# Feed-forward chunks of a four-layer trunk: the narrow chunk moved to the front, all five wide chunks in seven block products

## The chip, the cores and the metric

The kernel runs on one core of one Trainium2 chip. The metric is device time in microseconds (us), lower is better. A core has five engines that run their own instruction streams in order: PE (matmul; its weight loads, PEld, overlap it), DVE (element-wise, two tensors in), ACT (element-wise, one tensor in), POOL and SP; here POOL and SP mainly issue DMAs. What is queued on an engine behind a waiting instruction waits too.

## What is computed

A trunk of four layers on 256 tokens of width 1024, all in float32. Each layer is a feed-forward block (FFN), an attention block and a second FFN; so there are eight FFNs, and the change touches only them. Cut to that:

```
D_MODEL = 1024; SEQ = 256; DEPTH = 4; D_FF = 2816

def swiglu(x, w_in, w_out):
    gate, up = jnp.split(x @ w_in, 2, axis=-1)
    return (jax.nn.silu(gate) * up) @ w_out

for i in range(DEPTH):
    h = h + 0.5 * rms_norm(swiglu(rms_norm(h, g[0]), ffn_w_in[i, 0], ffn_w_out[i, 0]), g[1])
    ... attention: h = h + rms_norm(m, g[3])
    h = h + 0.5 * rms_norm(swiglu(rms_norm(h, g[4]), ffn_w_in[i, 1], ffn_w_out[i, 1]), g[5])
return h
```

## The kernel before

**Three passes for one product.** PE multiplies in a reduced form of float32 (fp32r), so every operand is split into a high part `hi` and a remainder `lo`, and a product is summed from three passes: x_hi·w_hi, x_hi·w_lo, x_lo·w_hi (`product`, L152; in the output products L244 to L246). The split of a weight unit of 128x2048 elements is one cast on ACT (L156, `hi`) and one subtraction on DVE (L157, `lo`). Weights come by DMA into "raw" tiles (nine, `RAWS`), and the split pairs stand in a ring of four (`UNITS`).

**Tokens.** The 256 tokens are two tiles, t=0 and t=1. Before an FFN each tile's normalized input (`xg`) is turned on PE (L181, `tpx`) and split into `xh` (ACT) and `xl` (DVE); ACT also copies the turned tile back (L184).

**Chunks.** The 2816 hidden columns are done in six chunks: five of 512 and one of 256. A chunk needs, for gate and up and for both token tiles, a product over the 1024 inputs. `plain` does these four products as they stand: 96 matmuls, of 512 or 256 columns. `wino` does the 2x2x2 block product (two token tiles, two input halves, gate and up) in seven block products of 12 matmuls (84) after Strassen and Winograd. For it, four sums of x (L271 to L274, `early`) and sums of the four weight quarters b00, b01, b10, b11 are formed: two of the weight sums on DVE (L372, 128x2048 each), two by accumulating DMAs that POOL issues (L375). The products of a wino chunk come in the order b00, b10, t2, t1, t3, b11, t4, into three PSUM banks `pb`, `pa`, `pc`; ACT copies the running sums out of `pb` (L492, L504, L509), DVE adds `pa` and `pc` (L487) and forms the gated value `g` (L431). `g` is turned (L439, `tpg`), split into `gh` (ACT) and `gl` (DVE), and multiplied into the output sums `y` one chunk later.

**Order before.** Chunk 0 is a plain 512, chunk 1 the plain 256, chunks 2 to 5 are wino 512s. The turn of token tile 1 (`turn_x`) stands in the second product of chunk 0, and the sums of x follow its third. The order in which each engine meets the instructions is set by a scheduler that works from its own estimates, not by the program text; so it is read from the built program.

The FFNs are called FFN 1 to FFN 8 in the order in which they run. FFN 3, 5 and 7 follow an FFN, FFN 2, 4, 6 and 8 an attention.

Of the kernel before, what the change touches and what calls it, by code (L numbers as in the profile page):

```python
# [9 lines left out]
F32 = mybir.dt.float32  # L10
# [26 lines left out]

RAWS = 9
UNITS = 4
WINO = (2, 3, 4, 5)  # L40

IN_NAMES = ["x", "norm_g", "ffn_w_in", "ffn_w_out", "diff_w_in", "diff_w_out", "diff_lambda",
            "diff_subln", "moba_w_in", "moba_w_out", "nsa_w_in", "nsa_w_out", "nsa_cmp_pe",
# [3 lines left out]
class Trunk:  # L47
# [235 lines left out]
    def ffn(self, l, f, X, ahead, end):  # L283
        nc = self.nc
        with self.tc.tile_pool(name=f"ffn{l}{f}", bufs=2, reuse_waits="tile") as pool:
            w_in, w_out = self.a["ffn_w_in"][l, f], self.a["ffn_w_out"][l, f]
            chunks = [(c, 512) for c in range(0, D_FF - 256, 512)]
            chunks.insert(1, (D_FF - 256, 256))
            last = len(chunks) - 1
            y = [None, None]  # L290
            G, U = {}, {}
# [45 lines left out]
            def close(n):  # L337
                U.pop(n)
                live["unit"] -= 1
# [19 lines left out]
            def plan_wino(j):  # L359


                c0, w = chunks[j]
                name = lambda n: (j, n)
                quarter = lambda k, u: (w_in, k * 512, 4, u * D_FF + c0, w)
                c1, w1 = chunks[j - 1]
                ko = [((j - 1, "o", k), (w_out, c1 + k * P, 2, 0, D)) for k in range(0, w1 // P, 2)]
                for n, src in ((name("b00"), quarter(0, 0)), (name("b01"), quarter(0, 1)),
                               (name("b10"), quarter(1, 0)), (name("b11"), quarter(1, 1)), (name("t2"), None), *ko):
                    loads.append(lambda n=n, src=src: raw(n, src))

                def add(to, a, b):
                    nc.vector.tensor_tensor(R[name(to)], R[name(a)], R[name(b)], op=ALU.add)  # L372

                def add_by_dma(to, b):
                    nc.gpsimd.dma_start(R[name(to)], R[name(b)], accum_op=ALU.add)  # L375

                def quarters(n, then=()):
                    split(name(n), name(n))
                    for x in then:
                        (add if len(x) == 3 else add_by_dma)(*x)  # L380

                def last_of(n, of, gone=None):
                    split(name(n), name(of), True)
                    if gone:
                        free(name(gone))

                outs = [lambda n=n: split(n, n, True) for n, _ in ko]

                def split_t2():
                    add("t2", "b00", "b11")  # L390
                    quarters("t2", [("t2", "b10")])

                preps.extend([
                    lambda: quarters("b00"),
                    lambda: quarters("b10", [("b00", "b00", "b01"), ("b01", "b11")]),
                    outs[0],
                    split_t2,
                    lambda: last_of("t1", "b00"),
                    lambda: last_of("t3", "b01"),
                    lambda: last_of("b11", "b11")])  # L400
                if j < last:
                    preps.extend(outs[1:])
                preps.append(lambda: last_of("t4", "t2", "b10"))
                if j == last:
                    preps.extend(outs[1:])

# [45 lines left out]
            def plain(j, order, between=()):  # L452
# [4 lines left out]
                for i, (which, t) in enumerate(order):  # L457
                    ns = [(j, "gu"[which], h) for h in hs]
                    ps = bank("ps")
                    for h, n in zip(hs, ns):  # L460
                        self.product(ps[:, :w], X[t][0], [(4 * h, unit(n))], h == 0, h == hs[-1])
                        if i == 1:
                            self.turn_x()
                    if which == 0:
                        sl[t] = gate(t, ps, w, j)
                    else:
                        up(t, ps, w, sl[t], j, X[t][1])
                    if (which, 1 - t) in order[:i]:
                        for n in ns:
                            close(n)  # L470
                    fill()
                    if between:
                        between.pop(0)()

            def wino(j):
# [9 lines left out]

                tile = lambda tag, t: pool.tile([P, 512], F32, tag=tag, name=f"{tag}{l}{f}_{j}_{t}")
                add = lambda d, x: nc.vector.tensor_tensor(d, x, d, op=ALU.add)  # L487
                s24, s31 = SUMS
                B = bank("pb")
                times(B, X[0][0], 0, "b00", True)  # L490
                sl0 = tile("sl", 0)
                nc.scalar.copy(sl0, B)  # L492
                fill()
                turn(j - 1, 0)
                A = bank("pa")
                times(A, X[0][0], 4, "b10", True)
# [47 lines left out]
                    nc.vector.tensor_scalar(r, X[t][1], -1.0, None, op0=ALU.mult)  # L544
                    nr.append(r)

            plain(0, [(0, 0), (1, 0), (0, 1), (1, 1)], [lambda: None, lambda: None, early])
            zig = [(0, 0), (0, 1), (1, 0), (1, 1)]
            for j in range(1, last + 1):
                if j in WINO:  # L550
                    wino(j)
                    continue
                plain(j, zig, [lambda: turn(j - 1, 0), lambda: turn(j - 1, 1)])
                for t in range(NT):
                    out(j - 1, t, (0, 2))
                for k in (0, 2):
                    close((j - 1, "o", k))
                fill()
                del G[j - 1, 0], G[j - 1, 1]
            turn(last, 0)  # L560
            out(last - 1, 0, (2,))
            ahead()
# [768 lines left out]
```

## Time and profile before

| | before |
|---|---|
| median of 3 runs | 1992.58 us (1991.72 to 1995.25) |
| the profiled execution, its own time | 1992.68 us |
| its span in the profile | 1991.0 us |
| PE busy | 1934.5 us (97%) |
| DVE busy | 1610.7 us (81%) |
| ACT busy | 1261.7 us (63%) |
| granted TensorE clock, mean | 0.999 |

The span is what the profile shows of one execution; 1.7 us of the execution's time lie around it. An engine's share is a mean over stages: PE can be the limit in one stretch and wait in another, and the stages of one FFN are told apart by time below.

### The profile page before, as it was taken

The page shows a single profiled execution, that of the slowest core. Times are in us where ns is not written, and L with a number is a line of the kernel's source. Part 1 is how long each engine was busy: PE and PEld are TensorE (multiplying, and loading weights), DVE is VectorE, ACT ScalarE, POOL GpSimd, SP SyncE. Part 2 cuts the span into 40 slices and gives each one's busy share as a digit, 9 for nine tenths or more (in the row PEclk, how much of TensorE's full clock was granted, in tenths as well). Part 3 has the DMA queues.
Part 4 walks back from the last instruction along what each step waited for, and adds up shares of the span by engine and source line. Part 5 has one row for each costly group of instructions (what it writes and reads, how often), then busy time and mean ns, then how long its engine had stood idle before and what let it go on. Part 6 is the DMA issues. An engine that isn't in the chain of part 4 may idle for free.

```text
span 1991.0 us, 25740 instructions
## 1 busy us (share of the span) xinstructions
PE 1934.5 (97%) x9712; PEld 1582.6 (79%) x9712; DVE 1610.7 (81%) x2040; ACT 1261.7 (63%) x1721; POOL 187.2 (9%) x303
## 2 busy tenths in 40 slices
PE   7999999999999999999999998999999999999998
PEld 6788878788878878878887887678788788878787
DVE  6799678799789766789879977877998798678797
ACT  6566666566566666566656666865666567576564
POOL 0000210000000120000000032000000000210000
PEclk9999999999999999999999999999999999999999
DMA  9795638696787556587868775166879685638692
GB/s 359 215 281 161 211 118 314 162 283 209 258 238 236 182 191 212 189 246 232 291 199 244 210 205 165 58 242 191 238 214 322 177 285 161 202 106 306 176 289 64
DMA packets 177867, 430.25 MB, mean 216 GB/s; under 512 B 8784, under 2 KB 37712, under 8 KB 169552
## 3 DMA queue, kind: packets, MB, share of 16 engines
q1 hardware_dynamic: 168528, 361.51, 50.7%
q0 software_dynamic: 9216, 67.11, 18.1%
q8 instruction: 76, 1.25, 0.3%
q14 instruction: 47, 0.39, 0.1%
HBM read 360.43 MB, written 1.05 MB: 182 GB/s over the span
## 4 chain that ended last, share of the span: by engine, by line
PE 66%; DVE 11%; issue 10%; DMA 6%; ACT 4%; POOL 0%; POOLq 0%; DVEq 0%; ACTq 0%
PE pb L152 12%; PE ps L152 8%; PE y L244 7%; PE y L246 7%; PE y L245 7%; PE pc L152 6%; DVE lo L157 5%; PE pw L675 4%; DMA raw<-raw 4%; PE pw L677 4%; PE pw L676 3%; PE pa L152 3%; ACT hi L156 2%; DMA raw<-in_ffn_w_in 2%; DVE raw L372 2%
## 5 line engine op out<-in xcount | busy, mean ns | idle before, releaser
L157 DVE TENSOR_TENSOR lo<-raw,hi 128x2048 fp32r<-128x2048 f32 (+3 forms) x534 | 981.0, 1862 | 227.1 <-ACT hi L156 226.5
L156 ACT CAST hi<-raw 128x2048 fp32r<-128x2048 f32 (+3 forms) x534 | 818.9, 1560 | 327.0 <-PE y L246 168.9
L244 PE MATMUL y<-hi,gh 128*128 128x512 f32 x704 | 278.5, 396 | 0.0
L245 PE MATMUL y<-lo,gh 128*128 128x512 f32 x704 | 274.4, 390 | 0.0
L246 PE MATMUL y<-hi,gl 128*128 128x512 f32 x704 | 267.4, 393 | 0.0
L152 PE MATMUL ps<-hi,xh 128*128 128x256 f32 (+1 forms) x512 | 175.4, 343 | 1.9 <-ACT xh L156 1.3
L152 PE MATMUL ps<-lo,xh 128*128 128x256 f32 (+1 forms) x512 | 173.1, 338 | 0.2 <-DVE lo L157 0.2
L152 PE MATMUL ps<-hi,xl 128*128 128x256 f32 (+1 forms) x512 | 172.9, 338 | 0.0
L675 PE MATMUL pw<-hi,xh 128*128 128x512 f32 (+2 forms) x432 | 164.6, 381 | 0.0
L152 PE MATMUL pb<-lo,sh 128*128 128x512 f32 x384 | 153.4, 400 | 5.7 <-DVE lo L157 5.7
L677 PE MATMUL pw<-hi,xl 128*128 128x512 f32 (+2 forms) x432 | 155.7, 360 | 0.0
L676 PE MATMUL pw<-lo,xh 128*128 128x512 f32 (+2 forms) x432 | 155.4, 360 | 0.0
L375 POOL DMA_DIRECT2D raw<-raw x64 | 55.5, 868 | 1059.7 <-DVE raw L372 506.9
L246 PEld LDWEIGHTS y<-hi,gl 128*128 128x128 f32 x704 | 131.6, 188 | 29.1 <-DVE gl L157 1.5
L152 PE MATMUL pb<-hi,sh 128*128 128x512 f32 x384 | 153.5, 400 | 0.5
L244 PEld LDWEIGHTS y<-hi,gh 128*128 128x128 f32 x704 | 132.3, 188 | 27.1 <-ACT gh L156 1.2
L245 PEld LDWEIGHTS y<-lo,gh 128*128 128x128 f32 x704 | 132.4, 188 | 26.3
L152 PE MATMUL pb<-hi,sl 128*128 128x512 f32 x384 | 150.2, 391 | 0.0
L372 DVE TENSOR_TENSOR raw<-raw,raw 128x2048 f32<-128x2048 f32 x64 | 146.3, 2286 | 0.3
L152 PEld LDWEIGHTS ps<-hi,xh 128*128 128x128 f32 x512 | 97.6, 191 | 13.1 <-ACT xh L156 2.2
L152 PEld LDWEIGHTS ps<-lo,xh 128*128 128x128 f32 x512 | 97.7, 191 | 11.2 <-DVE lo L157 1.1
L152 PEld LDWEIGHTS ps<-hi,xl 128*128 128x128 f32 x512 | 97.4, 190 | 11.1 <-DVE xl L157 1.1
(213 smaller groups left out, 3301.4 us busy)
## 6 DMA issues: line engine op xcount, KB each, us to landing
raw<-in_ffn_w_in SPq DMA_DIRECT2D x172, 1024.0 KB, 8.9
raw<-in_ffn_w_out SPq DMA_DIRECT2D x88, 1024.0 KB, 9.7
raw<-raw POOLq DMA_DIRECT2D x64, 1024.0 KB, 8.1
raw<-in_diff_w_in SPq DMA_DIRECT2D x24, 1024.0 KB, 5.3
raw<-in_moba_w_in SPq DMA_DIRECT2D x12, 1024.0 KB, 5.1
raw<-in_nsa_w_in SPq DMA_DIRECT2D x9, 1024.0 KB, 5.1
raw<-in_diff_w_out SPq DMA_DIRECT2D x8, 1024.0 KB, 4.9
gpre<-in_norm_g SPq DMA_DIRECT2D x12, 512.0 KB, 6.3
```

Of the source, the lines that this page charges most:

```text
L152: nc.tensor.matmul(out, l, r, start=first and i == 0, stop=last and i == len(steps) - 1, skip_group_check=more)
L156: self.nc.scalar.copy(hi, src)
L157: self.nc.vector.tensor_tensor(lo, src, hi.bitcast(F32), op=ALU.subtract)
L244: nc.tensor.matmul(y[b], x[0][:, kt, :], hi[:, k, s], start=f, stop=False)
L245: nc.tensor.matmul(y[b], x[0][:, kt, :], lo[:, k, s], start=False, stop=False)
L246: nc.tensor.matmul(y[b], x[1][:, kt, :], hi[:, k, s], start=False, stop=l)
L372: nc.vector.tensor_tensor(R[name(to)], R[name(a)], R[name(b)], op=ALU.add)
L375: nc.gpsimd.dma_start(R[name(to)], R[name(b)], accum_op=ALU.add)
L675: nc.tensor.matmul(out, x[0][:, kt, :], hi[:, k, :], start=first and i == 0, stop=False)
L676: nc.tensor.matmul(out, x[0][:, kt, :], lo[:, k, :], start=False, stop=False)
L677: nc.tensor.matmul(out, x[1][:, kt, :], hi[:, k, :], start=False, stop=last and i == len(todo) - 1)
```

## The change

The 256-wide chunk becomes chunk 0 and the only plain one; chunks 1 to 5 are wino. `wino` becomes a generator: the first product of chunk 1 (b00 with token tile 0) is issued between the second and the third product of the plain chunk, ahead of `turn_x` and of the sums of x. The weight sum t1 = b00 + b01 goes into a raw tile of its own instead of over b00, t2 is formed over b00 and t4 from it, and the two accumulating DMAs are placed accordingly. The order of loads is b00, b01, b11, b10.

```diff
-WINO = (2, 3, 4, 5)
+WINO = (1, 2, 3, 4, 5)
...
-            chunks.insert(1, (D_FF - 256, 256))
+            chunks.insert(0, (D_FF - 256, 256))
...
-                for n, src in ((name("b00"), quarter(0, 0)), (name("b01"), quarter(0, 1)),
-                               (name("b10"), quarter(1, 0)), (name("b11"), quarter(1, 1)), (name("t2"), None), *ko):
+                for n, src in ((name("b00"), quarter(0, 0)), (name("b01"), quarter(0, 1)), (name("t1"), None),
+                               (name("b11"), quarter(1, 1)), (name("b10"), quarter(1, 0)), *ko):
...
+                def first():
+                    split(name("b00"), name("b00"))
+                    add("t1", "b00", "b01")
+                    add_by_dma("b01", "b11")
+
+                def second():
+                    add("b00", "t1", "b11")
+                    split(name("t2"), name("b00"))
+                    add_by_dma("b00", "b10")
+
+                def fourth():
+                    split(name("t4"), name("b00"), True)
+                    free(name("b10"))
...
-                    lambda: quarters("b00"),
-                    lambda: quarters("b10", [("b00", "b00", "b01"), ("b01", "b11")]),
+                    first,
+                    lambda: split(name("b10"), name("b10")),
                     outs[0],
-                    split_t2,
-                    lambda: last_of("t1", "b00"),
-                    lambda: last_of("t3", "b01"),
-                    lambda: last_of("b11", "b11")])
+                    second,
+                    lambda: split(name("t1"), name("t1"), True),
+                    lambda: split(name("t3"), name("b01"), True),
+                    lambda: split(name("b11"), name("b11"), True)])
...
-                        if i == 1:
-                            self.turn_x()
...
-                s24, s31 = SUMS
                 B = bank("pb")
                 times(B, X[0][0], 0, "b00", True)
-                sl0 = tile("sl", 0)
+                sl0 = tile("sl", 0) if j > 1 else self.work.tile([P, D], F32, tag="yg", name=f"sl{l}{f}_1_0")[:, :512]
                 nc.scalar.copy(sl0, B)
                 fill()
+                if j == 1:
+                    yield
+                s24, s31 = SUMS
...
-            plain(0, [(0, 0), (1, 0), (0, 1), (1, 1)], [lambda: None, lambda: None, early])
-            zig = [(0, 0), (0, 1), (1, 0), (1, 1)]
-            for j in range(1, last + 1):
-                if j in WINO:
-                    wino(j)
-                    continue
...
+            first = wino(1)
+
+            def begin():
+                next(first)
+                self.turn_x()
+                early()
+
+            plain(0, [(0, 0), (1, 0), (0, 1), (1, 1)], [lambda: None, begin])
+            self.drain(first)
+            for j in range(2, last + 1):
+                self.drain(wino(j))
```

**What moves on the engines.** Three places follow; the numbers in the names only tell tiles apart. The first is DVE in FFN 3 from the input of token tile 1 (`xg`, L227) to its remainder `xl`. Before, four rows of work stand between them (`lo` of two half units and small ones, `st`):

```order
L227 TENSOR_TENSOR xg_4201<-h_89,gpre_4063 128x512 x2
L204 TENSOR_SCALAR st_4209<-st_4207 128x1
L157 TENSOR_TENSOR lo_4266<-raw_4229,hi_4265 128x1024
L206 SCALAR_TENSOR_TENSOR st_4214<-st_4212,st_4209 128x1
L157 TENSOR_TENSOR lo_4266<-raw_4229,hi_4265 128x1024
L544 TENSOR_SCALAR st_4394<-st_4130 128x1
L544 TENSOR_SCALAR st_4396<-st_4216 128x1
L157 TENSOR_TENSOR xl_4200<-tpx_4311,xh_4199 128x512
L157 TENSOR_TENSOR xl_4200<-tpx_4319,xh_4199 128x512
L271 TENSOR_TENSOR xg_4201<-xg_4201 128x512
```

Now the same stretch of DVE in FFN 3 (raw_4259 is t1 of chunk 1, raw_4255 its b00, lo_4290 the split of b10, lo_4362 that of the first output unit):

```order
L227 TENSOR_TENSOR xg_4229<-h_89,gpre_4091 128x512 x2
L204 TENSOR_SCALAR st_4237<-st_4235 128x1
L372 TENSOR_TENSOR raw_4259<-raw_4255,raw_4257 128x2048
L206 SCALAR_TENSOR_TENSOR st_4242<-st_4240,st_4237 128x1
L157 TENSOR_TENSOR lo_4290<-raw_4262,hi_4289 128x2048
L430 SCALAR_TENSOR_TENSOR g_0_0_4344<-ps_4319,st_4158,sl_0_0_4317 128x256
L372 TENSOR_TENSOR raw_4255<-raw_4259,raw_4260 128x2048
L157 TENSOR_TENSOR lo_4362<-raw_4264,hi_4361 128x2048
L157 TENSOR_TENSOR xl_4228<-tpx_4367,xh_4227 128x512
L157 TENSOR_TENSOR xl_4228<-tpx_4375,xh_4227 128x512
```

Four operations of 128x2048 now stand ahead of `xl`, where two of 128x1024 stood. The second place is ACT in the first wino chunk of FFN 3, from the split of `gh` of the second token tile on (`sl_2_1` takes the running sum out of `pb` after product t2). Before, in chunk 2:

```order
L156 CAST gh_1_1_4688<-tpg_1_1_4685 128x256
L504 COPY sl_2_1_4716<-pb_4637 128x512
L156 CAST hi_4718<-raw_4263 128x2048
L156 CAST hi_4736<-raw_4271 128x2048
L509 COPY g_2_1_4756<-pb_4637 128x512
```

Now, in chunk 1 of FFN 3 on ACT (hi_4530 is b11, hi_4550 t4, hi_4572 the next chunk's b00):

```order
L156 CAST gh_0_1_4498<-tpg_0_1_4495 128x256
L503 COPY sl_1_1_4528<-pb_4346 128x512
L156 CAST hi_4530<-raw_4260 128x2048
L497 ACTIVATE sl_1_0_4359<-sl_1_0_4359,st_4158 128x512
L156 CAST hi_4550<-raw_4255 128x2048
L508 COPY g_1_1_4570<-pb_4346 128x512
L156 CAST hi_4572<-raw_4266 128x2048
```

The order around the copy is the same, with the gate's activation moved behind it; what has changed is how late the product comes for which the copy waits. The third place is DVE in chunk 4 of FFN 2, behind the sum of `pa` (`sl_4_0`); every FFN has the same rows. Before:

```order
L157 TENSOR_TENSOR gl_3_0_3680<-tpg_3_0_3674,gh_3_0_3679 128x512
L487 TENSOR_TENSOR sl_4_0_3666<-pa_3683,sl_4_0_3666 128x512
L157 TENSOR_TENSOR lo_3649<-raw_3482,hi_3648 128x2048
L157 TENSOR_TENSOR lo_3669<-raw_3350,hi_3668 128x2048
L157 TENSOR_TENSOR lo_3699<-raw_3352,hi_3698 128x2048
```

Now, in the same chunk 4 on DVE (raw_3658 is t1 of chunk 5, lo_3676 the split of t2 of chunk 4):

```order
L157 TENSOR_TENSOR gl_3_0_3707<-tpg_3_0_3701,gh_3_0_3706 128x512
L484 TENSOR_TENSOR sl_4_0_3693<-pa_3710,sl_4_0_3693 128x512
L372 TENSOR_TENSOR raw_3658<-raw_3588,raw_3590 128x2048
L157 TENSOR_TENSOR lo_3676<-raw_3368,hi_3675 128x2048
L157 TENSOR_TENSOR lo_3696<-raw_3438,hi_3695 128x2048
```

The next chunk's weight sum has come in ahead of the split of t2.

## Rows read from the trace of the kernel before

**Rows 1.** The page's first part: busy time, share of the span, instructions.
```profile
PE 1934.5 (97%) x9712; PEld 1582.6 (79%) x9712; DVE 1610.7 (81%) x2040; ACT 1261.7 (63%) x1721; POOL 187.2 (9%) x303
```

**Rows 2.** Groups by line and shape, whole span: busy, mean ns, idle before.
```profile
L157 DVE TENSOR_TENSOR lo<-raw,hi 128x2048 fp32r<-128x2048 f32 x328 | 741.7, 2288 | 163.7 <-ACT hi L156 163.7
L156 ACT CAST hi<-raw 128x2048 fp32r<-128x2048 f32 x328 | 618.3, 1906 | 270.5 <-PE y L246 155.1 <-DMA raw<-raw 32.3 <-issue 27.4
...
L372 DVE TENSOR_TENSOR raw<-raw,raw 128x2048 f32<-128x2048 f32 x64 | 146.3, 2286 | 0.3
```

**Rows 3.** FFN 3 in three windows: length, PE, PEld, DVE, ACT, POOL busy, clock.
```profile
496.20:541.00 44.80, 44.80 (x252) 39.29 (x251) 33.69 (x38) 25.23 (x30) 2.81 (x3) 1.00 0.88 299
541.00:589.00 48.00, 44.70 (x198) 35.18 (x197) 41.45 (x26) 29.40 (x26) 2.58 (x3) 1.00 0.67 178
589.00:624.00 35.00, 35.00 (x158) 28.59 (x157) 31.18 (x20) 24.35 (x20) 1.72 (x2) 1.00 0.91 283
```

**Rows 4.** PE, timeline (start, length): FFN 3, marked products.
```profile
496.22 0.39 PE L152 MATMUL ps<-hi,xh 128*128 128x512 f32 x1
...
504.39 1.04 PE L181 MATMUL tpx<-ident,xg 128*128 128x128 f32 x8
...
519.00 0.28 PE L152 MATMUL ps<-lo,xh 128*128 128x256 f32 x1
519.12 0.28 PE L152 MATMUL ps<-hi,xl 128*128 128x256 f32 x1
...
589.21 0.39 PE L152 MATMUL pc<-hi,sh 128*128 128x512 f32 x1
```

**Rows 5.** DVE, timeline at the start of FFN 3, token tile 1.
```profile
500.88 1.28 DVE L227 TENSOR_TENSOR xg<-h,gpre 128x512 f32<-128x512 f32 x2
...
505.64 1.29 DVE L157 TENSOR_TENSOR xl<-tpx,xh 128x512 fp32r<-128x512 f32 x2 [0.48 <-ACT xh L156]
507.59 0.69 DVE L271 TENSOR_TENSOR xg<-xg 128x512 f32<-128x512 f32 x1 [0.66 <-ACT xg L184]
```

**Rows 6.** DVE groups by shape, FFN 3 (496.2 to 624 us): short operations.
```profile
L157 DVE TENSOR_TENSOR sl<-xg,sh 128x1024 fp32r<-128x1024 f32 x2 | 2.4, 1220 | 0.0
...
L431 DVE SCALAR_TENSOR_TENSOR g<-pb,st,sl 128x512 f32<-128x512 f32 x2 | 1.5, 748 | 0.0
...
L431 DVE SCALAR_TENSOR_TENSOR g<-ps,st,sl 128x256 f32<-128x256 f32 x2 | 1.0, 480 | 0.0
```

**Rows 7.** DVE, timeline in chunk 4 of FFN 2 (a settled wino chunk).
```profile
426.41 0.69 DVE L157 TENSOR_TENSOR gl<-tpg,gh 128x512 fp32r<-128x512 f32 x1
427.01 0.68 DVE L487 TENSOR_TENSOR sl<-pa,sl 128x512 f32<-128x512 f32 x1
427.87 6.70 DVE L157 TENSOR_TENSOR lo<-raw,hi 128x2048 fp32r<-128x2048 f32 x3 [0.17 <-ACT hi L156]
```

**Rows 8.** PE, timeline in the same chunk 4 of FFN 2.
```profile
427.10 0.48 PE L244 MATMUL y<-hi,gh 128*128 128x512 f32 x1
...
429.96 0.39 PE L152 MATMUL pb<-hi,sh 128*128 128x512 f32 x1
430.21 0.50 PE L152 MATMUL pb<-lo,sh 128*128 128x512 f32 x1
```

**Rows 9.** PE, waits of FFN 3's third chunk (timeline, waiting rows).
```profile
571.71 0.66 PE L439 MATMUL tpg<-ident,g 128*128 128x128 f32 x4 [1.25 <-DVE g L431]
577.37 0.66 PE L439 MATMUL tpg<-ident,g 128*128 128x128 f32 x4 [1.34 <-DVE g L431]
```

**Rows 10.** PE, timeline of the kernel's first matmuls after the wait for the input.
```profile
15.06 0.63 PE L152 MATMUL ps<-hi,xl 128*128 128x512 f32 x1
15.49 0.63 PE L152 MATMUL ps<-hi,xh 128*128 128x512 f32 x1
...
16.41 0.39 PE L152 MATMUL ps<-hi,xh 128*128 128x512 f32 x1
16.64 0.40 PE L152 MATMUL ps<-lo,xh 128*128 128x512 f32 x1
```

More of the change, by code (lines that the diff above doesn't have):

```diff
@@ L375, in add_by_dma @@
                     nc.gpsimd.dma_start(R[name(to)], R[name(b)], accum_op=ALU.add)
[L377 to L385, printed above, removed]
+                def first():
[9 more added lines that the diff above has]
+                    free(name("b10"))
                 outs = [lambda n=n: split(n, n, True) for n, _ in ko]
-                def split_t2():
-                    add("t2", "b00", "b11")
-                    quarters("t2", [("t2", "b10")])
                 preps.extend([
-                    lambda: quarters("b00"),
-                    lambda: quarters("b10", [("b00", "b00", "b01"), ("b01", "b11")]),
+                    first,
+                    lambda: split(name("b10"), name("b10")),
                     outs[0],
-                    split_t2,
-                    lambda: last_of("t1", "b00"),
-                    lambda: last_of("t3", "b01"),
-                    lambda: last_of("b11", "b11")])
+                    second,
+                    lambda: split(name("t1"), name("t1"), True),
+                    lambda: split(name("t3"), name("b01"), True),
+                    lambda: split(name("b11"), name("b11"), True)])
                 if j < last:
                     preps.extend(outs[1:])
-                preps.append(lambda: last_of("t4", "t2", "b10"))
+                preps.append(fourth)
                 if j == last:
@@ L545, in early @@
                     nr.append(r)
-            plain(0, [(0, 0), (1, 0), (0, 1), (1, 1)], [lambda: None, lambda: None, early])
-            zig = [(0, 0), (0, 1), (1, 0), (1, 1)]
-            for j in range(1, last + 1):
-                if j in WINO:
-                    wino(j)
-                    continue
[L553 to L559, printed above, removed]
+            first = wino(1)
[7 more added lines that the diff above has]
+                self.drain(wino(j))
             turn(last, 0)
```

## The prediction

> **What bounds the kernel now.** I read the page's busy times first [rows 1]. PE is busy 97% of the span, so a removed matmul can pay directly, but DVE at 81% is the next engine; whether a saving survives depends on where inside an FFN DVE has room. The groups by shape give the prices [rows 2]: a 128x2048 remainder or weight sum costs DVE 2.29 us, and 2.20 us when several stand in a row (three take 6.70, [rows 7]); a cast costs ACT 1.91 us. Then I cut FFN 3 into windows [rows 3]. In its first 44.8 us PE never waits and DVE has only 33.7 us of work: chunk 0 and chunk 1 are plain, long on PE and light on DVE. In the next 48.0 us PE loses 3.3 us, part of it in two waits for the gated value [rows 9]. In the last 35.0 us PE is full again and DVE has 31.2 us. So the FFN lives on a stock of prepared weights that the slow plain chunks let DVE and ACT build up.
>
> A settled wino chunk is 84 block matmuls, 48 output matmuls and 8 turns. Starts are 0.227 us apart for 512 columns ([rows 10] at the end, 0.23), so 132 x 0.227 + 8 x 0.11 = 30.9 us, 31.2 with the small waits I read in such chunks. It runs without slack at one point: `gl` ends at 427.1, the output product starts at 427.10, product t2 at 429.96, its second matmul needs the remainder of t2 and starts at 430.21 [rows 8]; the first of the three remainders ends at 427.87 + 2.2 = 430.1 [rows 7]. The lead of DVE there is 0.1 us.
>
> **The change part by part.**
>
> *PE.* In each FFN one plain 512 chunk of 96 matmuls becomes 84: 12 x 0.227 = 2.7 us, and 8 x 2.72 = 21.8 us in all. The 256 chunk costs the same wherever it stands (96 matmuls 0.12 us apart [rows 4], 11.5 us). If nothing else moved the result would be 1992.7 - 21.8 = 1970.9.
>
> *DVE and ACT.* Seven products need seven weight units where the plain chunk needs four: three more casts (3 x 1.91 us on ACT) and three more remainders, plus two weight sums, on DVE 5 x 2.20 = 11.0 us, plus about four short PSUM sums less two gates, some 2 us: 13 us of DVE work per FFN, against 2.7 us less of PE. And the cover goes. Before, PE had 21.8 + 11.5 + 10.9 us (512 chunk, 256 chunk, 48 output matmuls) until the first wino product; now it has half a 256 chunk, 5.8 us, and the b00 product, 2.7 us, before it needs token tile 1.
>
> *The start of an FFN, worked for FFN 3.* Mark: the start of product t3 in the second wino chunk. Before it is at 589.21, 93.0 us after the first product at 496.22 [rows 4]. Two chunks follow before, three after the change, so after minus before is (mark + 31.2) - 93.0.
> Token tile 1's input is ready at 500.88 + 1.28 = 502.2 [rows 5]. After the change a 2048-wide split of b00 stands ahead of tile 0's turned halves on ACT and DVE where a 1024-wide one stood, which I follow through to 503.6.
> From there DVE runs, in the new order, up to `gl` of chunk 1: ten remainders and four sums, 14 x 2.20 = 30.8 us. Eighteen short ones: two gates of 256 (0.48 each), two `xl` (0.65), four sums of x (0.69), two `sl` (1.22), two `gl` of 256 (0.42), three PSUM sums (0.69), two gates of 512 (0.75), one `gl` of 512 (0.69), 12.6 us [rows 5, 6], less 0.07 of overlap each, 11.3; tiny ones 0.2. Together 42.3 us of DVE with no gap.
> The gaps: 0.6 us for ACT's copy of the turned tile, as before [rows 5]; 1.3 for the cast of t2, since its slot comes free only after the plain chunk's third product, which itself waits for `xl`; 0.2 for a cast of the sums; 2.3 for the cast of b11, which stands on ACT behind the copy of the sum after t2, and t2's product ends at about 529.7 because the output matmuls amid it wait for the `gl` of the 256 chunk, which DVE ends at about 526.7; 2.6 for the cast of t4, whose slot the last output matmul of the 256 chunk frees at about 535; 0.3 at the next cast. Sum 7.3.
> So `gl` ends at 503.6 + 42.3 + 7.3 = 553.2. From `gl` to t3 it is 2.9 us to t2 as in [rows 8] and 36 matmuls, 8.2: the mark is at 564.3, 68.1 us after the FFN's start, and 68.1 + 31.2 - 93.0 = **+6.3 us**. The old chunk 2 to 3 transition with its waits [rows 9] is inside the 93.0; it does not vanish, it moves into the new chunks 1 and 2. Seen from PE: it stands about 2 us for the late `xl` of tile 0, 6 for that of tile 1, 4 for the first `gl`, 3 for the second, 15 us, where it stood some 5.5.
> FFN 2, followed the same way with its own order, gives +6.8; the others have the same row pattern, FFN 1 with smaller units. I take 6.3 x 8 = **+50**. Bounds: if the three cast waits of 1.3, 2.3 and 2.6 all vanish, +0.1 per FFN, +1; if every hop between engines that I took as free costs 0.1 to 0.2 us over some ten hops, +8, +64.
>
> *The hoisted sum.* In chunk 4 of each FFN the sum for chunk 5 now stands between the `pa` sum and the remainder of t2. That remainder comes 2.20 us later with a lead of 0.1; PE fills 0.23 with a matmul of t3 that is placed there. 2.20 - 0.1 - 0.23 = 1.9, say 1.8 for the 0.2 us that DVE waits for ACT at that place before [rows 7]: 8 x 1.8 = **+14**. Bounds: 0, if DVE is ahead by then; +18 with the whole 2.20.
>
> *Nothing.* The accumulating DMAs are as many as the sums need and start from the same queue; the seven loads that stand ahead of the new chunk 1's last quarter are those that stood there before, and land before DVE reaches them by the chain above. Were one late, the chain would wait for it directly.
>
> Sum against the profiled execution, 1992.68, which is the median of 1992.58 within 0.1: 1992.7 + 50 + 14 = **2057**. The 21.8 us of PE are inside the +50 already.
>
> **A rule weighed.** The first matmuls after the wait for the input are 0.43 us apart instead of 0.227, ten of them, of which the last pair stands in [rows 10]: the lower of the two clocks (1.2 for 2.4 GHz), although PEclk in the windows reads 1.00 [rows 3]. Each new FFN start has one PE wait of about 6 us and three of 2 to 4. If ten spacings after each 6 us wait are slow, that is 10 x 0.2 = 2 us x 8 = 16; if the 4 us wait counts too, 32. Where PE then still waits for DVE it is free. The Trainium skill, TensorE: Matmul & The Clock Gate, section "HAM oscillation — how this bites in real kernels", says that an idle array falls back to half clock and is slow again at the next burst. By that rule alone the sum would be up to 2073 or 2089; the trace has no wait that long inside the kernel, so it decides nothing here.
>
> **The rivals.**
> (a) *Faster: the seven-product chunk pays.* For that the DVE chain from tile 1's input to `gl` must shrink from 49.6 to under 43.3 us; that is break-even. Its work alone is 42.3, so six of its seven us of gaps would have to go, or the first rows run before the input is there. For it: DVE has 11.1 us to spare in the first window and 6.6 in the second [rows 3], which an order with the sums earlier could use; against it: the new order puts them behind tile 1's input. With chain and hoisted sum free, 1971; with the chain part free, 1975 to 1988. Chance 0.07.
> (b) *No net change*, gaps nearly gone and the hoisted sum half hidden: 1989 to 1997. Chance 0.03.
> (c) *Softer start.* The casts of b11 and t4 come in time, because tiles are freed earlier than I follow, and half the cast waits go (-3 x 8), or the hoisted sum is hidden (-14): 2005 to 2040. Chance 0.22.
> (d) *Clock.* The waits above bring the half clock and it is not hidden: 2075 to 2095. Chance 0.13.
> Forecast, 2040 to 2075: chance 0.55.
>
> **How the numbers follow.** Faster by over 0.2% (4 us, about what a measurement of this kernel can tell from no change) is (a), 0.07; within it (b), 0.03; slower the rest, 0.90. The range leaves out (a), (b), the low part of (c) and the upper half of (d), about 0.2: 2018 to 2082.
>
> **What would show it.** Right: in FFN 3 a PE wait of 5 to 6 us for `xl` of tile 1 just after the turn, 4 us for `gl` before the first output product, and the mark near 68 us after the start; in chunk 4 of each FFN a wait of PE's `pb` (lo pass) on DVE of about 1.8 us; PE busy down by about 22 us while the span grows by 64. Wrong: PE waits in the first 60 us of an FFN below 9 us in sum; the t2 remainder of chunk 4 in time; rows of PE at 0.43 us spacing inside FFNs would point to (d).

## The result and the profile after

| | before | after |
|---|---|---|
| median | 1992.87 us (1991.72 to 1995.25) | 2044.01 us (2039.89 to 2047.05) |
| ratio, with its 95% interval | | 1.0254 (1.0233 to 1.0274) |
| span of the profiled execution | 1991.0 us | 2045.1 us |
| mean granted TensorE clock | 0.999 | 0.983 |

The change makes the kernel 51 us slower. The forecast was 2057, inside 2018 to 2082, with 0.90 on slower.

First the page of after and its groups by shape, the same views as [rows 1, 2]:

```profile
PE 1938.2 (95%) x9616; PEld 1587.1 (78%) x9616; DVE 1711.1 (84%) x2092; ACT 1319.4 (65%) x1757; POOL 199.4 (10%) x319
```
```profile
L157 DVE TENSOR_TENSOR lo<-raw,hi 128x2048 fp32r<-128x2048 f32 x368 | 833.1, 2286 | 129.9 <-ACT hi L156 129.3
...
L372 DVE TENSOR_TENSOR raw<-raw,raw 128x2048 f32<-128x2048 f32 x80 | 182.6, 2282 | 0.1
```

PE has 96 matmuls fewer, as counted, and DVE 100 us more work: 40 remainders of this shape and 16 sums more. The first surprise is that PE's busy time did not fall by 22 us; it rose by 4. The PE waits of after (who waits and for whom: sum, number, longest) come next, then those of before.

```profile
PE ps L152 <- DVE xl L157: 24.4, 12, 3.2
PE ps L152 <- ACT xh L156: 15.3, 8, 2.1
PE pc L152 <- ACT hi L156: 14.0, 8, 1.8
PE tpg L438 <- DVE g L430: 10.0, 8, 2.8
```
```profile
PE tpg L439 <- DVE g L431: 20.8, 17, 1.3
```

With the groups that are not shown, PE's waits inside the eight FFNs sum to 79.4 us after and 29.0 before: +50.4. The 96 matmuls that are gone are worth 96 x 0.227 = 21.8. The span grew by 54.1, so some 54.1 - 50.4 + 21.8 = 25.5 us more are unexplained by waits: PE was busy, but slower. Where is seen in the second FFN below.

The start of FFN 3 on PE (timeline: start, length, in brackets the wait before) and on DVE, to be held against [rows 4, 5]:

```profile
512.72 0.28 PE L152 MATMUL ps<-hi,xh 128*128 128x256 f32 x1
...
525.84 0.39 PE L152 MATMUL ps<-hi,xh 128*128 128x256 f32 x1 [2.09 <-ACT xh L156]
...
529.26 0.58 PE L152 MATMUL ps<-hi,xl 128*128 128x256 f32 x1 [2.91 <-DVE xl L157]
...
540.48 0.48 PE L244 MATMUL y<-hi,gh 128*128 128x512 f32 x1
540.80 0.39 PE L245 MATMUL y<-lo,gh 128*128 128x512 f32 x1
...
579.16 0.39 PE L152 MATMUL pc<-hi,sh 128*128 128x512 f32 x1
```
```profile
519.26 2.28 DVE L372 TENSOR_TENSOR raw<-raw,raw 128x2048 f32<-128x2048 f32 x1
...
521.53 2.28 DVE L157 TENSOR_TENSOR lo<-raw,hi 128x2048 fp32r<-128x2048 f32 x1
...
524.12 2.28 DVE L372 TENSOR_TENSOR raw<-raw,raw 128x2048 f32<-128x2048 f32 x1
526.32 2.28 DVE L157 TENSOR_TENSOR lo<-raw,hi 128x2048 fp32r<-128x2048 f32 x1
528.52 1.28 DVE L157 TENSOR_TENSOR xl<-tpx,xh 128x512 fp32r<-128x512 f32 x2
...
536.41 2.29 DVE L157 TENSOR_TENSOR lo<-raw,hi 128x2048 fp32r<-128x2048 f32 x1 [3.08 <-ACT hi L156]
...
551.36 4.58 DVE L157 TENSOR_TENSOR lo<-raw,hi 128x2048 fp32r<-128x2048 f32 x2 [2.12 <-ACT hi L156]
...
567.19 0.68 DVE L157 TENSOR_TENSOR gl<-tpg,gh 128x512 fp32r<-128x512 f32 x1
```

The four rows of 2.28 us stand ahead of `xl`, as the built order said, and PE waits 2.91 for it. The marked product t3 starts at 579.16, 66.4 us after the FFN's first matmul. Against the forecast's 31.2 us per later chunk and the 93.0 of before [rows 4], that is +4.6 us. The same sum over all eight FFNs, each with its own two marks, gives 9.4, 4.8, 4.6, 3.8, 4.7, 3.6, 4.4 and 4.1: +39.4 us (FFN 1 has the first). Closing FFN 3: +4.6 at its start, +1.9 in chunk 4, -0.1 in chunk 5, -0.3 at its end, +6.1; its length to the last output matmul went from 181.8 to 187.9.

Most of the 25 us of slower PE show at the starts of the FFNs; here FFN 2. These are its windows, with the columns of [rows 3] (window; length; PE, PEld, DVE, ACT, POOL busy; granted clock; DMA share and GB/s), and rows of PE's timeline in them:

```profile
337.20:341.00 3.80, 1.87 (x9) 1.66 (x10) 3.80 (x6) 1.51 (x3) 0.00 (x0) 0.73 1.15 211
341.00:345.00 4.00, 4.00 (x20) 4.00 (x20) 3.90 (x5) 0.30 (x1) 0.00 (x0) 0.50 0.73 263
```
```profile
337.10 0.39 PE L152 MATMUL ps<-hi,xh 128*128 128x256 f32 x1 [2.09 <-ACT xh L156]
...
339.54 0.58 PE L152 MATMUL ps<-hi,xl 128*128 128x256 f32 x1 [1.93 <-DVE xl L157]
...
341.20 0.41 PE L152 MATMUL ps<-hi,xh 128*128 128x256 f32 x1
341.41 0.41 PE L152 MATMUL ps<-lo,xh 128*128 128x256 f32 x1
...
345.84 0.28 PE L152 MATMUL ps<-lo,xh 128*128 128x256 f32 x1
345.96 0.28 PE L152 MATMUL ps<-hi,xl 128*128 128x256 f32 x1
```

After two waits of about 2 us, with only two matmuls between them, PE has work without a break. Yet its matmuls of 256 columns start 0.21 us apart and not 0.12, and the granted clock is 0.50 for four microseconds: the lower of the two levels, 1.2 GHz. It lasts here for 29 matmuls and costs them some 2.8 us. The other FFNs have 16 to 27 such late starts: FFN 1, with matmuls of 512 columns, some 3.4 us, the others 1.9 to 2.6, about 20 of the 25 us in all eight; FFN 5 has 1.6 us more in its chunk 4. The Trainium skill, TensorE: Matmul & The Clock Gate, section "HAM oscillation — how this bites in real kernels", describes an array that falls to half clock in one long wait and starts the next burst cold; this trace agrees on the cold burst, with the 0.50 above, but here there were two shorter waits with two matmuls between them.

The third place, chunk 4 of FFN 2, on DVE, ACT and PE, to be held against [rows 7, 8]:

```profile
442.69 2.28 DVE L372 TENSOR_TENSOR raw<-raw,raw 128x2048 f32<-128x2048 f32 x1
444.89 6.69 DVE L157 TENSOR_TENSOR lo<-raw,hi 128x2048 fp32r<-128x2048 f32 x3
```
```profile
445.23 1.88 ACT L156 CAST hi<-raw 128x2048 fp32r<-128x2048 f32 x1
```
```profile
422.55 0.39 PE L152 MATMUL pc<-lo,sh 128*128 128x512 f32 x1
...
447.17 0.50 PE L152 MATMUL pc<-hi,sh 128*128 128x512 f32 x1 [1.75 <-ACT hi L156]
...
447.50 0.39 PE L152 MATMUL pb<-lo,sh 128*128 128x512 f32 x1
...
455.56 0.39 PE L152 MATMUL pc<-lo,sh 128*128 128x512 f32 x1
```

The sum has come in ahead of the three remainders, and PE stands 1.75 us. The wait is put down to the cast for the first matmul of t3 (`pc`), which the new order places ahead of the lo pass of t2. That cast ends at 445.23 + 1.88 = 447.11, and the remainder of t2, with which DVE is late, at 444.89 + 2.2 = 447.1: the row alone does not tell which of the two held PE. From the t3 of chunk 3 to that of chunk 4, by the second matmul of each (422.55 and 455.56), it is 33.0 us and not 31.2.

### The profile page after: what moved, and what is told of

Its sections match the earlier page's. It is cut to its first block, busy times and chain, and to the rows that moved or that the text cites. A ratio compares the mean times of both kernels' runs of the same rounds, so it can differ in the third digit from the quotient of the medians.

```text
span 2045.1 us, 25757 instructions
## 1 busy us (share of the span) xinstructions
PE 1938.2 (95%) x9616; PEld 1587.1 (78%) x9616; DVE 1711.1 (84%) x2092; ACT 1319.4 (65%) x1757; POOL 199.4 (10%) x319
## 4 chain that ended last, share of the span: by engine, by line
PE 65%; DVE 17%; ACT 8%; issue 7%; POOL 1%; DMA 1%; SPq 0%; DVEq 0%; ACTq 0%; POOLq 0%
PE pb L152 16%; DVE lo L157 8%; PE pc L152 7%; PE y L246 7%; PE y L244 7%; PE y L245 7%; ACT hi L156 6%; DVE raw L372 4%; PE pw L672 4%; PE pw L674 3%; PE pw L673 3%; PE ps L152 3%; PE pa L152 3%; PE tpg L438 1%; PE sc L746 1%
## 5 line engine op out<-in xcount | busy, mean ns | idle before, releaser
L157 DVE TENSOR_TENSOR lo<-raw,hi 128x2048 fp32r<-128x2048 f32 (+3 forms) x546 | 1034.1, 1918 | 191.6 <-ACT hi L156 190.3
L156 ACT CAST hi<-raw 128x2048 fp32r<-128x2048 f32 (+3 forms) x546 | 865.3, 1607 | 261.0 <-PE y L246 144.7
L152 PE MATMUL pb<-hi,sh 128*128 128x512 f32 x480 | 190.2, 396 | 0.0
L152 PE MATMUL pb<-hi,sl 128*128 128x512 f32 x480 | 187.9, 392 | 0.6 <-DVE sl L157 0.6
L152 PEld LDWEIGHTS pb<-lo,sh 128*128 128x128 f32 x480 | 90.4, 188 | 29.9 <-DVE lo L157 12.4
L152 PEld LDWEIGHTS pb<-hi,sh 128*128 128x128 f32 x480 | 90.3, 188 | 24.0 <-ACT sl L503 5.7
L152 PEld LDWEIGHTS pb<-hi,sl 128*128 128x128 f32 x480 | 90.4, 188 | 19.9 <-DVE sl L157 1.0
L152 PE MATMUL ps<-hi,xl 128*128 128x256 f32 x256 | 81.4, 322 | 24.4 <-DVE xl L157 24.4
L757 ACT ACTIVATE e<-e,st 128x128 f32<-128x128 f32 (+1 forms) x160 | 71.7, 450 | 40.6 <-DVE st L754 39.7
L119 POOL TENSOR_TENSOR st<-st,negh 128x1 f32<-128x1 f32 (+1 forms) x56 | 48.2, 860 | 504.1 <-DVE st L206 431.4
```

The costliest lines, as they stand in the source:

```text
L152: nc.tensor.matmul(out, l, r, start=first and i == 0, stop=last and i == len(steps) - 1, skip_group_check=more)
L156: self.nc.scalar.copy(hi, src)
L157: self.nc.vector.tensor_tensor(lo, src, hi.bitcast(F32), op=ALU.subtract)
L757: nc.scalar.activation(e[:, c, :], e[:, c, :], AF.Exp, scale=-1.0, bias=top[:, c:c + 1], accum_out=tot[:, c:c + 1])
```

## Experiments

The theory: PE's saving is real, but at an FFN's start DVE (and a little ACT) is the bound, so that it is swallowed; the hoisted sum adds some 2 us per FFN; and the clock adds a part. The rivals: the mere order (narrow chunk first) costs the time, whatever the number of products; or a wait at one place, which another order would cure, and not the sum of DVE's work.

### Three suspected terms, one by one

**e1_sum_behind** holds the hoisted sum of chunk 5 back until the remainder of chunk 4's b11 is made:

```diff
...
-                    add("t1", "b00", "b01")
+                    if j == last:
+                        with self.tc.issue_after(LO[j - 1, "b11"]):
+                            add("t1", "b00", "b01")
+                    else:
+                        add("t1", "b00", "b01")
```

> The changed kernel with one order edge more: in chunk 4 of each FFN the weight sum for chunk 5 may not be issued before the remainder of b11. My theory: the hoisted sum costs 1.8 us in each of 8 FFNs, so this one is 14 us shorter than the changed kernel (about 2030), and the steps from t3 of chunk 3 to t3 of chunk 4 fall from 33.3 to 31.2 us. Rival, that the sum only shifts a wait that is paid later in the chunk: within 4 us of the changed kernel (2044).

Measured: 2025.34 us, 18.7 below the change. DVE and PE in chunk 4 of FFN 2:

```profile
439.75 6.69 DVE L157 TENSOR_TENSOR lo<-raw,hi 128x2048 fp32r<-128x2048 f32 x3 [0.17 <-ACT hi L156]
```
```profile
442.10 0.50 PE L152 MATMUL pb<-lo,sh 128*128 128x512 f32 x1
```

This is [rows 7, 8] again: the remainders follow the `pa` sum, PE has no wait before the lo pass, and t3 to t3 is 31.2 us. PE's order has changed back with it, the t3 matmul behind the lo pass; the run takes out the sum and this matmul together. The hoisted sum is shown, at 1.9 us per FFN by t3 to t3, 15 in all. That the run gains 18.7 has other parts: in the two profiled executions 1.5 us lie in chunk 4 of FFN 5, where the change has a stretch of half clock, and 0.1 per FFN in chunk 5; the rest is not placed.

**e6_filler** gives PE throw-away matmuls of 512 columns to do while it waits for `xl`, ahead of the plain chunk's third product; their bank is overwritten by it:

```diff
+FILL = 18
...
+                    while idle:
+                        idle.pop()
+                        for _ in range(FILL):
+                            nc.tensor.matmul(ps, X[0][0][0][:, 0, :], X[0][0][0][:, :4, :], start=True, stop=True,
+                                             skip_group_check=True)
...
+                idle.append(True)
```

> The changed kernel with 18 matmuls of 512 columns whose results are thrown away, put on PE right behind the turn of token tile 1, where it stands for xl for 4.4 to 5.6 us in every FFN. My theory: about 30 matmuls of 256 columns after that wait ran 0.213 us apart instead of 0.12, they end 2.9 us earlier if the clock is kept, of which about 1.8 us were in DVE's wait for the cast of t2; so about 14 us less than the changed kernel (2030), and no stretch below granted clock 0.9 there. Rival, that DVE sets the pace and the low clock is hidden: within 4 us of 2044, or above it if the fillers themselves stand in the way.

Measured: 2029.43 us, 14.6 below the change, with a mean clock of 0.997. The second of the windows of FFN 2, behind the fillers:

```profile
341.00:345.00 4.00, 4.00 (x35) 4.00 (x34) 3.90 (x6) 2.48 (x3) 0.00 (x0) 1.00 0.73 267
```

No useful work was taken away and some useless was added, and the kernel got faster; in this window PE does 35 matmuls where it did 20. By name and shape DVE's 2092 rows stand in the order of the change, so no new order on DVE made the gain. So the half clock is real: the filler takes away some 20 us of late starts, and 14.6 us arrived.

**e8_behind_and_filler** has both edits.

> The changed kernel with both the order edge of e1 (19 us less) and the filler matmuls of e6 (15 us less). If the two losses are separate, they add up: 2044 - 19 - 15 = 2010. Rival, that both are the same wait seen twice: 2025.

Measured: 2012.22 us, 31.8 below the change; 18.7 + 14.6 = 33.3, so the two terms add. Some 19 us above before are left, with 21.8 us of matmuls less.

### The parts of the change alone

**e2_order_only** is the kernel before with its narrow chunk in front and four wino chunks; the sums as before:

```diff
-            chunks.insert(1, (D_FF - 256, 256))
+            chunks.insert(0, (D_FF - 256, 256))
...
-                    out(j - 1, t, (0, 2))
-                for k in (0, 2):
+                    out(j - 1, t, (0,))
+                for k in (0,):
```

> The kernel before with only the chunk order changed: the plain 256 first, the plain 512 second, then four wino chunks; nothing is added on DVE. My theory, that the extra weight preparation and the lost stock of time make the loss: only the wait for the turned second token tile comes earlier (5.8 us of PE work before it instead of 10.9), some 1 to 3 us per FFN, so 2000 to 2017. Rival, that the narrow chunk in front is itself the loss: over 2025.

Measured: 1990.86 us, ratio 0.9991 (0.9982 to 1.0001): no cost. This is below the band that I expected. The order does bring waits at the start, the largest in the PE waits of this kernel being

```profile
PE tpx L181 <- DVE xg L227: 12.2, 7, 2.8
...
PE ps L152 <- DVE xl L157: 8.7, 11, 1.5
```

but the waits for `g` between the last plain and the first wino chunk [rows 9], 20.8 us in all before, are gone in return. The rival "the order costs the time" falls.

**e3_own_tile_only** is the kernel before with the new way of summing: t1 in a tile of its own, t2 over b00, loads in the order b00, b01, b11, b10 (the hunks from `loads` to `preps` of the change).

> The kernel before, chunk order and all, with only the new preparation of the weight sums (t1 in a tile of its own, t2 over b00, loads in the new order). My theory: the same number of remainders, sums and DMAs in much the same places, so 1993 within 4 us. Rival, that the tile of its own takes a raw buffer and delays loads or sums: 2000 or more.

Measured: 1973.07 us, ratio 0.9903 (0.9888 to 0.9917): 20 us faster than before, where I had expected none. It is the fastest kernel of the study. From t3 of chunk 2 to t3 of chunk 3 it takes 27.3 us and before 30.0, in every FFN. POOL, then ACT's cast of t4 in FFN 3; in each fence before's row is the first, e3's the second:

```profile
551.31 0.86 POOL L375 DMA_DIRECT2D raw<-raw  x1 [16.96 <-DVE lo L157]
542.74 0.86 POOL L375 DMA_DIRECT2D raw<-raw  x1 [33.99 <-DVE lo L157]
```
```profile
559.56 1.91 ACT L156 CAST hi<-raw 128x2048 fp32r<-128x2048 f32 x1 [3.33 <-DMA raw<-raw]
552.45 1.91 ACT L156 CAST hi<-raw 128x2048 fp32r<-128x2048 f32 x1 [0.33 <-PE y L246]
```

Before, t1 overwrites b00, so it must wait for b00's split, t2 for t1, and the accumulating DMA for t2's split; ACT waits 3.33 us for that DMA, and 3.3 to 3.5 in the other FFNs. With t1 apart DVE sums it early, in the stock-building plain chunks (13.3 us after the FFN's start and not 34.6), and the DMA goes out 50.8 us after the start (491.96) and not 55.1 (496.22). ACT's wait for it at this place is gone in all eight FFNs.

**e11_tile_old_loads** is e3 with the old order of loads, so that b11 comes last of the four quarters:

```diff
-                for n, src in ((name("b00"), quarter(0, 0)), (name("b01"), quarter(0, 1)), (name("t1"), None),
-                               (name("b11"), quarter(1, 1)), (name("b10"), quarter(1, 0)), *ko):
+                for n, src in ((name("b00"), quarter(0, 0)), (name("b01"), quarter(0, 1)), (name("b10"), quarter(1, 0)),
+                               (name("b11"), quarter(1, 1)), (name("t1"), None), *ko):
```

> As e3 (kernel before, only the new preparation of the sums; it measured 1973), but with the loads in the old order: b10 ahead of b11, and the tile for the sum taken last. If the tile of its own is what removes the waits of the third chunk, it stays at 1973. If the earlier load of b11 does it, it goes back towards 1993.

Measured: 1980.49 us, ratio 0.9936 (0.9919 to 0.9952), between the two answers: 12.0 us below before, and 7.4 above e3. That the 7.4 are the earlier b11's is not shown. In FFN 2 to 8 the step from t3 of chunk 2 to t3 of chunk 3 is 27.3 us, as in e3; in FFN 1 alone it is 30.0, and ACT's wait is there again:

```profile
79.28 1.90 ACT L156 CAST hi<-raw 128x2048 fp32r<-128x2048 f32 x1 [3.32 <-DMA raw<-raw]
```

The two profiled executions are 8.5 us apart. Of that 3.0 lie in FFN 1; 3.1 between FFN 5 and FFN 6, in an attention block, where the granted clock of e11 reads 0.50 in windows (1205 to 1208.4 us, 1219 to 1222) and e3's does not; 0 to 0.7 in each other FFN. So the tile of its own is what removes the wait in seven FFNs, and the earlier b11 matters in the first.

**e7_order_and_tile** has both parts, order and tile, and four wino chunks.

> The change without its fifth seven-product chunk: narrow chunk first, sums with the tile of its own, and the first wide chunk (chunk 1) in plain products. The order alone measured 2 us under before, the tile alone 20 us under; if the two add up, 1971, and the fifth seven-product chunk then costs 73 us against it. Rival, that the loss comes from the narrow chunk in front together with the new preparation: 2010 or more.

Measured: 1989.75 us, ratio 0.9984 (0.9974 to 0.9994): a miss. The 20 us of the tile do not come on top of the order's 2; in the new order the tile is worth 1 us. The reason is in e2's trace: with the narrow chunk in front the DMA goes out 48.7 us after the start of FFN 3, earlier than in e3, and ACT does not wait for it before the cast of t4, in any FFN:

```profile
550.68 1.91 ACT L156 CAST hi<-raw 128x2048 fp32r<-128x2048 f32 x1 [0.33 <-PE y L246]
```

So the order alone cures that wait, and there is little left there for the tile. In FFN 3, 5 and 7 e7 is 0.5 to 0.9 us shorter than e2; in FFN 4 and 6 it is 2.9 and 1.1 longer, and there its granted clock falls for a stretch in which e2's does not. By e7, the fifth chunk in seven products, with its filling of the start, costs 2044.0 - 1989.8 = 54 us, although it takes 21.8 us of matmuls away.

### What binds the start

All four have the hoisted sum out of the way, as in e1; e9 and e12 stand on e8 and have its filler too.

**e9_no_sums_in_chunk_1** forms no weight sums on DVE in chunk 1 (two per FFN); t1 is split from b01, t2 from b00 as it is:

```diff
-                        add("t1", "b00", "b01")
+                    elif j > 1:
+                        add("t1", "b00", "b01")
...
-                    add("b00", "t1", "b11")
+                    if j > 1:
+                        add("b00", "t1", "b11")
...
-                    lambda: split(name("t1"), name("t1"), True),
+                    lambda: split(name("t1"), name("t1"), True) if j > 1 else nosum(),
```

> As e8, and the two weight sums of chunk 1 on DVE are left out (t1 is split from b01, t2 from b00, so that chunk's result is another); all splits and DMAs stay. My theory, that the DVE chain sets the pace of an FFN's start: 2 x 2.20 us less in each of 8 FFNs, 35 us under e8. Rival, that PE or the casts on ACT set it: within 8 us of e8.

Measured: 2000.96 us, 11.3 below e8 and not 35. Two sums of 2.20 us are 4.4 per FFN; 1.4 arrived. In FFN 3, DVE has a new wait, for the cast of the first output unit; ACT in front of that cast waits 3.31 us for PE's b00 product, as it does in the change:

```profile
513.98 2.29 DVE L158 TENSOR_TENSOR lo<-raw,hi 128x2048 fp32r<-128x2048 f32 x1 [2.83 <-ACT hi L157]
```

So 2.83 of the 4.4 us lay in the shadow of another chain, PE to ACT to DVE, of nearly the same length.

**e10_turn_first** lets tile 1 go first: the turn and the sums of x, and only behind `xl` the first sum of weights and the b00 product. It has no filler. Against e1:

```diff
...
+                    if j > 1:
+                        add_by_dma("b01", "b11")
+                    else:
+                        late.append(lambda: (add("t1", "b00", "b01"), add_by_dma("b01", "b11")))
...
             def begin():
-                next(first)
                 self.turn_x()
+                xl = self.lo_ins.ins
                 early()
+                with self.tc.issue_after(xl):
+                    late.pop()()
+                    next(first)
```

> As e1, and token tile 1 is turned ahead of the first product of chunk 1, with the weight sums of chunk 1 and the first output unit's split issued on DVE behind xl. The same work in another order. My theory: PE has 2.7 us of work while tile 1 is split, the wait that lowers the clock goes, and DVE's wait of 3.1 us for the cast of t2 goes with it: e1 measured 2025, less 15 for the clock and 1 to 2 us per FFN, 1995 to 2003. Rival, that only the sum of DVE's work counts: 2010, as for e8.

Measured: 2013.23 us (2006.17 to 2014.57), a miss: 12 below e1, but no gain over e8's 2012.22. The PE waits:

```profile
PE pb L152 <- DVE lo L157: 15.7, 17, 2.0
PE tpg L448 <- DVE g L440: 11.1, 9, 1.5
...
PE pb L152 <- ACT sh L156: 6.9, 5, 1.8
PE ps L152 <- DVE xl L157: 6.8, 7, 1.2
```

The wait for `xl` fell from 24.3 us in e1 to 6.8. Others took its place, later in the same chain: for the cast of the sums of x (`sh`), none in e1; for remainders into `pb`, 9.2 in e1, the growth mostly at the b00 product of chunk 2; and for the gated value, which now comes 22 us after the start of FFN 3, 5 and 7. But the mean clock was 0.990, so the half clock was back, at another place, and the comparison with e8 was not clean.

**e14_turn_first_filler** therefore adds throw-away matmuls to e10 around that place, six and six, into the bank that t3 overwrites:

```diff
...
+                if j == 1:
+                    C = bank("pc")
+                    filler(C)
                 turn(j - 1, 1)
                 o(0, 0)
+                if j == 1:
+                    filler(C)
                 times(B, s24, 0, "t2", False)
```

> As e10, with throw-away matmuls in PE's two waits before the first t2 product: six of 512 columns ahead of the turn of the second gated tile, six ahead of t2 (each six 1.36 us, the waits 1.4 each in e10). e10 had a mean clock of 0.990 and read 0.50 to 0.82 in windows behind these waits, so its 2013 may hide a gain. Theory (DVE's work bounds the start, the slow matmuls of e10 mostly fill PE's waits for DVE): 2008 to 2014, no better than e8 with its 2012, with the clock back at 0.996 or more. Rival (the turn first does shorten the start, and the half clock ate it): the slow stretches are worth about 0.007 x 2011 = 14 us of PE's time, some two thirds of it on the path, so 2000 to 2005.

Measured: 2007.27 us (2005.86 to 2008.61), clock 0.995. One window of FFN 3, in e10 and then in e14, and the fillers of e14:

```profile
528.00:532.00 4.00, 4.00 (x14) 3.12 (x14) 4.00 (x5) 0.73 (x1) 0.00 (x0) 0.75 1.01 166
```
```profile
528.00:532.00 4.00, 4.00 (x19) 3.27 (x18) 4.00 (x5) 0.88 (x1) 0.00 (x0) 1.00 1.04 197
```
```profile
526.92 3.00 PE L485 MATMUL pc<-xh 128*128 128x512 f32 x12 [1.40 <-DVE g L441]
```

The number lies between the two answers. The fillers do not stand in PE's waits: the twelve come together, behind the wait for the gated value, and reach into the window, so its 19 matmuls are not all useful ones. PE's order behind them and some casts on ACT moved too, and the clock still falls in FFN 4 and 7 (1539 to 1543 us reads 0.67). So the 6.0 us between e10 and e14 are not shown to be the half clock's alone. Against e8 this order, with its fillers, is worth some 5 us, 0.6 per FFN. The sizes are rough: the ratios to before are 1.0093 (1.0073 to 1.0112) for e10, 1.0094 (1.0079 to 1.0109) for e8 and 1.0072 (1.0054 to 1.0090) for e14, and their intervals overlap. DVE is busy through the whole of both windows.

**e12_out_before_t2** moves the output product of token tile 1 ahead of t2 in chunk 1, so that the slot for t4's cast comes free earlier:

```diff
+                if j == 1:
+                    o(1, 0)
...
-                o(1, 0)
+                if j > 1:
+                    o(1, 0)
```

> As e8 (2012), and in chunk 1 the output product of token tile 1 is written ahead of product t2, so that it frees its slot in the ring of four sooner. In e8 DVE waits 2.1 us per FFN for the cast of t4, which waits on ACT for that slot (2.4 us). My theory: that wait shrinks by 1 to 2 us in each of 8 FFNs, 1996 to 2004. Rival, that another wait takes its place, since DVE has no more slack: 2012 within 4.

Measured: 2013.19 us, as e8. DVE in FFN 3, e8's two rows and then e12's at the second of the places:

```profile
527.30 2.29 DVE L158 TENSOR_TENSOR lo<-raw,hi 128x2048 fp32r<-128x2048 f32 x1 [1.24 <-ACT hi L157]
...
542.24 4.58 DVE L158 TENSOR_TENSOR lo<-raw,hi 128x2048 fp32r<-128x2048 f32 x2 [2.13 <-ACT hi L157]
```
```profile
539.15 2.29 DVE L158 TENSOR_TENSOR lo<-raw,hi 128x2048 fp32r<-128x2048 f32 x1 [1.65 <-ACT hi L157]
541.80 2.29 DVE L158 TENSOR_TENSOR lo<-raw,hi 128x2048 fp32r<-128x2048 f32 x1 [0.36 <-ACT hi L157]
```

One wait of 2.13 became two of 2.01 in sum, and the mark stayed at 64.6 us. In e8 DVE waits 0.53 + 1.24 + 2.13 = 3.9 us in the 46.8 us from the input of tile 1 to `gl`.

No single wait sets the start. DVE is nearly full there, and where a wait or an operation goes, the next chain is 1 to 3 us behind: taking out 4.4 us of its work brought 1.4 (e9), another order about 0.6 (e14), an earlier cast nothing (e12). That DVE's work is the main bound fits all of these, but no run shows it alone. How the rest, 2007.3 - 1989.8 = 17.5 us against four seven-product chunks (e7), divides between its work and the hops between PE, ACT and DVE stays open.

## Why the prediction was right, and where its steps were off

- **PE -21.8, swallowed at the start.** Right that it is swallowed, and shown by e7 against the change (+54 with 96 matmuls less); of the 54, 18.7 are e1's, in chunk 4, and 14.6 the clock's (e6). Rivals (a) and (b), 0.10 together, fell: the chain that would have had to shrink below 43.3 us took 48.6, from 519.26 to 567.87.
- **The start, +50.** Measured +39.4. In FFN 3 the chain was forecast at 49.6 us, 42.3 of work and 7.3 of gaps; it had 42.9 of work and 5.7 of gaps, 0.53 + 3.08 + 2.12. The work was right. The failed step is the gap of 2.3 for the cast of b11, with the 4 us of PE's wait for the first `gl` behind it. The first output matmuls are the passes hi·gh and lo·gh, at 540.48 and 540.80 above, and the same two for the second half at 541.03 and 541.27; none of the four needs `gl`. PE had work, the copy of `pb` came in time, and the gap was 0. DVE also came into the chain 6.54 us after the FFN's first matmul (519.26 less 512.72) and not 7.4. What I got wrong: I took a wait of a product's third pass for a wait of the whole product.
- **The cast of t2, 1.3.** Mis-sized the other way: 3.08, because the half clock stretched the plain chunk's third product, which frees its slot. With the filler it is 1.24 (e8), the forecast's figure. The 1.8 us between the two, taken eight times, are near the 14.6 of e6.
- **The PE waits**, forecast as 2, 6, 4 and 3 us. For `xl` of tile 1 and its `xh` it is 2.09 + 2.91, near the 6; for the first `gl` none, for the others about 1 each. In the first 60 us of FFN 2 to 8 these waits sum to 7.0 to 7.9 us, below the 9 that the prediction itself had named as a sign of being wrong. The 5.5 us that it gives PE for before are 3.3 by [rows 3]; its sum does not use them.
- **The hoisted sum, +14.** Right in mechanism and near in size: 1.9 us of chunk 4 from t3 to t3 against 1.8, 15 in all. e1 gains 18.7, but not all of it in this step. One piece was wrong: PE's spare matmul of t3 saved nothing, since it waited for its own cast until 447.11.
- **Nothing, for the sums' new tile.** Near right for the new order, where e7 against e2 gives it 1 us, but for a reason that I did not have; with the fifth wino chunk no run tests it. In the old order it is worth 20 us with the new loads (e3), 12 with the old ones (e11). I priced the DMAs by their number and their queue, and not by when their inputs are ready; ACT's wait for it, 3.33 us in FFN 3, was in the trace of before, its sum of 32.3 even in [rows 2], and I had not read it.
- **The clock, rival (d), 0.13.** I had it as an excess that comes on top or not at all, with ten slow spacings after a long wait. It came, after two waits of 1.8 to 3.2 us with two matmuls between (FFN 2 to 8), for 19 to 29 matmuls; 14.6 us of it were on the path. Its chance was too low, and it belonged into the sum.

So the middle was 13 us high: -10.6 at the start, +2 in chunk 4, -2 in chunk 5 and at the end, where I had put nothing, and -3 because the profiled execution of after (2047.05 us) was that much above the median. The start's 39.4 contains most of the clock's cost, which I had left out of the sum; with the filler (e6) the same marks give 23 and not 50. Two errors cancel in part, and that the forecast is better than its parts is luck.

## What to carry to other kernels

A matmul saved pays only where the engines that prepare its operands have room in that very stretch: here 21.8 us of PE bought 54 us of loss. A sum of weights that slipped ahead made some 19 of them and the clock 15; the rest, some 20, fits that the seven-product chunk took the long plain products under which DVE had built its stock. A sum that overwrites its own input ties a whole chain (sum, next sum, DMA, cast) to the split of that input; giving it a tile of its own brought 0.6% where that chain was late (1.0% with the loads reordered), and 0.1% where it was not. And where PE has two waits close together, throw-away matmuls in them can be worth their place: 0.7% here.

## What the hardware showed that I had not expected

- After waits of 2.09 and 1.93 us, broken by two matmuls, the granted clock read 0.50 in the next window although PE worked there without a break; 29 matmuls of 256 columns ran 0.21 us apart instead of 0.12. Matmuls of no use in the wait kept the clock at 1.00.
- In FFN 5 it fell after a single wait, the 1.76 us of chunk 4: the window from 1127 to 1131 us reads 0.57, and matmuls of 512 columns start 0.43 us apart there. Behind the same wait in the other seven FFNs it stayed at 1.00.
- The mean clock of the execution, 0.983, hides it: it is one stretch of at least 6 us at the start of each FFN.
